# Moving the input norm of a hybrid encoder layer from the loads to the first two q tiles of group B

## Chip, cores, metric

The kernel runs on one core of one Trainium2 chip. The metric is the device time of one execution in microseconds (us), as the median of several runs.

## The reference

One layer of a streaming encoder. It is given 512 prompt tokens and 8 x 16 sample tokens (640 in all) of width 2048, caches of keys and values for the samples, and the weights. What matters for this change is its beginning:

```
def rmsnorm(x, g):
    xf = x.astype(jnp.float32)
    y = xf * lax.rsqrt(jnp.mean(xf * xf, axis=-1, keepdims=True) + EPS)
    return (y * g.astype(jnp.float32)).astype(x.dtype)

qa, ka, va, qb, kb, vb = split_proj(rmsnorm(x, norm_mix) @ w_in)
qb = rope_partial(qb, pos)
kb = rope_partial(kb, pos)
oa = band_attend(...)      # group A: 16 heads, learned bias
ob = band_attend(...)      # group B: 16 q heads, 2 kv heads, sinks
y = merge_and_ffn(x, oa, ob, ...)
```

The projection of a normed row is the projection of the row times its gain, scaled afterwards by one number for each token, r = 1/sqrt(mean(x^2) + EPS). So the projection can begin before r is known, and r is needed only when a projected tile is scaled. Behind the attention follow the output projection, a SwiGLU of width 5632 and a last norm.

## The kernel before

All activations are held with features on the 128 partitions and the 640 tokens along the free dimension, as two halves of 320. `xT` is 16 tiles of 128x640. Each operand of a dense product is split into two fp32r parts, a high one by ScalarE (L168 for weights, L172 for x with its gain) and a low one by VectorE (L169, L173), and each product is three matmuls: high by high (L177), high by low of one side (L178) and of the other (L179). In `dense` (L195) one output tile of 128x640 takes 16 k tiles x 2 halves x 3 = 96 matmuls of 128x320. It accumulates in a buffer of the PSUM pool "dn", of which there are two. A bank group is free for the next output once its result has been taken out. Weights come in chunks of up to 8 k tiles of 128x128: `weights` (L187) takes a raw slot (list WR, two slots), issues the load on SyncE's queue, and splits it into a slot for the high and one for the low part (list WH, four slots, so two chunks).

The program begins with the load loop (L319). It loads the 16 x tiles, splits them (`acts`), and between them loads the weights of k and v of group B (w_in 24 and 25) in three chunks each of 2, 6 and 8 k tiles. The k and v tiles are accumulated together (`dense(first, acts, 2)`), so they hold both "dn" buffers, and follow the loads k tile by k tile.

`input_norm` (L331) makes r: the raw x tiles are squared in place, the squares are added into one tile, TensorE sums them over partitions with a column of ones (L221), six small instructions make the inverse root with a Newton step, and TensorE spreads it over the partitions again (L233), from where ScalarE copies it into `r_mix` (L235). Before the change six of the 16 squares and five adds are GpSimd's (L335, L339), ten squares are ScalarE's (L337), and ten adds VectorE's (L341).

Work beside the dense products is written as generators in a queue ("heads"). `dense` calls `tick` after every six matmuls of an output, which adds `rate` to a counter and runs one step (`pump`) of the queue for each whole number. `rate` is 1.0 at first, 0.8 from the k and v tiles on, and 1.1 from p = 4, where the decoding of the samples joins as a second stream. `input_norm` is the first generator; `drain` (L103) runs it to its end behind the k and v product. The heads of the attention follow in the same queue, two at a time: scores of a pair (L367, L369), softmax, transposes (L289), products with v (L184, L185). Four steps make the scores of a pair, and there are some 18 steps in all. The matmuls of a step never stand ahead of the dense matmul that was written before them (`keep_pace`). For the rest a scheduler places instructions of independent chains on each engine; each engine then works off its queue in order.

After the k and v product come: `proj` (L352), which takes a result out of PSUM and scales it with `r_mix` in one VectorE instruction (L356); `rope` (L503), which zeroes a tile on GpSimd (L505), moves rows by four small DMAs (L507, L508), and adds up on VectorE (L509 to L511); the splits of k; the transposed v (`values`). Then the loop over p runs `project_b` twice (q tiles 26 + t) and `project_a` once (k, q, v of group A), for p = 0 to 3, and `project_a` alone for p = 4 to 7.

The lists S, W, F and others are slots of on-chip memory handed out by `get` and given back by `put`. `qps`, in the changed kernel, is a list of the two PSUM results that wait for their scale.

Of the kernel before, what the change touches and what calls it, by code (L numbers as in the profile page):

```python
# [7 lines left out]
AF = mybir.ActivationFunctionType  # L8
ALU = mybir.AluOpType
# [6 lines left out]
KT = 16  # L16
# [29 lines left out]
def halves(ap):  # L46
    return ap.rearrange("p (a b) -> p a b", a=2)
# [222 lines left out]
def build(nc, tc, io, pools):  # L270
    n = Net(nc, tc, io, pools)
# [26 lines left out]
    def pair(lst, k=TOK):  # L298
        a, b = n.get(lst), n.get(lst)
        return (a, b), (r(a[:, :k]), r(b[:, :k]))  # L300
# [9 lines left out]
    r_mix, cos, sin, kb0, kb1, vb0, vb1 = (n.get("C") for _ in range(7))  # L310
# [6 lines left out]
    xg, acts, xs = [], [], []  # L317
    first = []
# [10 lines left out]
        xs.append(xr)  # L329

    def input_norm():  # L331
        pool = (1, 3, 5, 7, 9, 11)
        for i, x in enumerate(xs):
            if i in pool:
                nc.gpsimd.tensor_tensor(x, x, x, ALU.mult)  # L335
            else:
                nc.scalar.activation(x, x, AF.Square)  # L337
        for i in pool[1:]:
            nc.gpsimd.tensor_tensor(xs[1], xs[1], xs[i], ALU.add)  # L339
        for i, j in ((0, 2), (4, 6), (8, 10), (0, 4), (12, 13), (0, 8), (0, 1), (14, 15), (0, 12), (0, 14)):  # L340
            nc.vector.tensor_tensor(xs[i], xs[i], xs[j], ALU.add)  # L341
        for _ in range(25):
            yield
        n.put("S", *xs)
        for _ in n.rstd_steps({a: [xs[0][:, a * HT:a * HT + HT]] for a in range(2)}, D, r_mix):
            for _ in range(4):
                yield
        n.move("S", "Q", 4)
        dma(out=cos[:80], in_=io["rope"][0])
        dma(out=sin[:80], in_=io["rope"][1])  # L350

    def proj(idx, ps=None):  # L352
        if ps is None:
            ps = n.dense([(io["w_in"][idx, :, k:k + 8], 8) for k in (0, 8)], acts)
        out = n.get("F")
        nc.vector.tensor_tensor(halves(out), ps, halves(r_mix), ALU.mult)  # L356
        return out
# [131 lines left out]
    def heads_of(kind, p, held, *args):  # L489
        ot = n.get("S")  # L490
        left = [2]

        def done():
            left[0] -= 1
            if not left[0]:
                dma(out=(oa_d if kind is prompt_a else ob_d)[p, :, :SP], in_=ot[:, :SP])
                n.put("S", ot)
                for lst, t in held:
                    n.put(lst, t)

        n.add("heads", kind(p, *args, ot, done))

    def rope(x):  # L503
        rot = n.get("S")
        nc.gpsimd.memset(rot[:80], 0.0)  # L505
        for b in (0, 64):
            dma(out=rot[b:b + 8], in_=x[b + 8:b + 16])  # L507
            dma(out=rot[b + 8:b + 16], in_=x[b:b + 8])  # L508
        nc.vector.tensor_tensor(x[:80], x[:80], cos[:80], ALU.mult)  # L509
        nc.vector.tensor_tensor(rot[:80], rot[:80], sin[:80], ALU.mult)  # L510
        nc.vector.tensor_tensor(x[:80], x[:80], rot[:80], ALU.add)  # L511
        n.put("S", rot)
# [170 lines left out]
        n.put("D", o_s, bias, *z, *held)  # L683


    n.add("heads", input_norm())
    ps_k, ps_v = n.dense(first, acts, 2)
    n.drain()
    n.rate = 0.8
    kf = proj(24, ps_k)  # L690
    rope(kf)
    dma(out=io["o_kb"], in_=kf)
    n.split(kf, *kb)
    n.put("F", kf)
    vf = proj(25, ps_v)
    dma(out=io["o_vb"], in_=vf)
    values(vf, [r(x[:, :SP]) for x in (vb0, vb1)])
    ps = n.bank()[:, :P]
# [2 lines left out]
    n.put("F", vf)  # L701

    def project_b(t):
        qf = proj(26 + t)
        rope(qf)
        nc.vector.tensor_scalar(qf, qf, 0.125, None, ALU.mult)
        dma(out=sb_d[:, t], in_=qf[:, SP:])
        qo, qb = pair("Q", SP)
        n.split(qf[:, :SP], *qb)
        n.put("F", qf)  # L710
        heads_of(prompt_b, t, [("Q", x) for x in qo], qb)
# [25 lines left out]
    for p in range(8):  # L737
        if p < 4:
            project_b(2 * p)
            project_b(2 * p + 1)  # L740
        if p == 4:
            while len(n.lists["Q"]) < 4:
                n.pump()
            n.move("Q", "D", 4)
            n.put("D", cos, sin)
            n.streams = (("heads 0", "heads"), ("decode", "decode"))
            n.add("decode", decode_b())
            n.add("decode", decode_a(0))
            n.rate = 1.1
        project_a(p)  # L750
# [24 lines left out]
    for m in range(KT):  # L775
        ps = n.dense([(io["w_out_b"][m], 8)], acts_b)
        if m == 0:
            n.rstd(ssq, 1024, r_b)
        xr, x = n.get("S"), n.get("S")
# [53 lines left out]
    for i, m in enumerate(m for kt in range(8) for m in (kt, kt + 8)):  # L833
        ps = n.dense([(io["w_out_a"][m], 8)], acts_a)
# [355 lines left out]
```

## Time and profile before

| | us |
|---|---|
| median of 3 runs | 2677.78 |
| the runs | 2683.37, 2677.60, 2677.78 |
| the profiled execution | 2685.62 |
| its span in the profile | 2683.8 |

The mean granted clock of TensorE in the profiled execution was 0.989. A row of a timeline reads: start in us from the span's start, duration, engine, line and operation, out<-in with shapes, count, and in brackets the idle time of the engine before it and what ended it. A row of the waits reads: who waited, for whom, us in total, times, longest. A row of the windows reads: stretch, its length, busy time and count of instructions of TensorE's matmuls, its weight loads, VectorE, ScalarE and GpSimd, then the granted TensorE clock, the DMA engines' busy share and GB/s. A merged row ("x4") gives the time from the first start to the last end; instructions of one engine overlap a little, so the spacing from start to start is shorter than the duration of one.

### The profile page before, as it was taken

What the parts mean: (1) busy time and instruction counts of PE and PEld (TensorE: products, weight loads), DVE (VectorE), ACT (ScalarE), POOL (GpSimd) and SP (SyncE); (2) the same over time, 40 slices, a digit from 0 to 9 for tenths busy, and PEclk for the clock granted to TensorE, in tenths of its full rate; (3) what the DMA queues carried; (4) which work ended last, traced back from release to release, by engine and by line L of the source; (5) the groups of instructions that cost most, each with busy time, mean ns of one, the idle gap of its engine ahead of it and who ended that gap; (6) DMA issues with size and microseconds to landing.
All of it is one profiled execution on the core that took longest, in us unless ns stands there. A gap on an engine that the chain in (4) does not pass through costs nothing.

```text
span 2683.8 us, 44823 instructions
## 1 busy us (share of the span) xinstructions
PE 2600.3 (97%) x17565; PEld 2540.1 (95%) x17565; DVE 1925.1 (72%) x2956; ACT 1081.2 (40%) x1759; POOL 789.5 (29%) x564
## 2 busy tenths in 40 slices
PE   7999999999999999999999999999999999999986
PEld 7999999899899999999999999999999899999986
DVE  7555566655866877667676667666678888888897
ACT  4333344434633643333333333333334444444443
POOL 3000000000302223333433433333335434344354
PEclk9999999999999999999999999999999999999998
DMA  5222223333655432332333333333325644444344
GB/s 162 89 72 89 96 66 105 119 120 130 214 188 194 152 123 96 109 117 97 120 104 112 118 104 106 116 106 105 121 96 174 216 132 127 130 133 129 108 114 139
DMA packets 154147, 332.23 MB, mean 124 GB/s; under 512 B 18064, under 2 KB 69264, under 8 KB 153936
## 3 DMA queue, kind: packets, MB, share of 16 engines
q1 hardware_dynamic: 153936, 329.38, 38.9%
q8 instruction: 138, 2.26, 0.4%
q14 instruction: 73, 0.60, 0.1%
HBM read 274.38 MB, written 54.20 MB: 122 GB/s over the span
## 4 chain that ended last, share of the span: by engine, by line
PE 84%; DVE 7%; DMA 3%; issue 3%; ACT 2%; POOL 0%; SPq 0%; DVEq 0%; ACTq 0%; POOLq 0%
PE dn L177 18%; PE dn L179 18%; PE dn L178 17%; PE at L177 9%; PE at L178 8%; PE at L179 8%; DVE W L169 2%; PE at L289 2%; PE at L367 1%; DVE S L908 1%; DMA W<-w_down 1%; DMA S<-act_d 1%; PE at L185 1%; PE at L184 1%; DVE S L1079 1%
## 5 line engine op out<-in xcount | busy, mean ns | idle before, releaser
L177 PE MATMUL dn<-S,W 128*128 128x320 f32 x3694 | 1164.0, 315 | 17.5 <-ACT S L920 7.1
L179 PE MATMUL dn<-S,W 128*128 128x320 f32 x3694 | 1149.6, 311 | 16.6 <-DVE W L169 16.5
L178 PE MATMUL dn<-S,W 128*128 128x320 f32 x3694 | 1148.3, 311 | 2.2 <-DVE S L173 1.1
L168 ACT ACTIVATE W<-W 128x1024 fp32r<-128x1024 f32 (+2 forms) x632 | 608.3, 964 | 1047.3 <-PE dn L178 524.7
L169 DVE TENSOR_TENSOR W<-W,W 128x1024 fp32r<-128x1024 f32 (+2 forms) x632 | 771.0, 1220 | 132.1 <-ACT W L168 128.3
L177 PEld LDWEIGHTS dn<-S,W 128*128 128x128 f32 x3694 | 698.7, 189 | 32.3 <-issue 9.5
L179 PEld LDWEIGHTS dn<-S,W 128*128 128x128 f32 x3694 | 698.4, 189 | 21.9 <-DVE W L169 21.2
L178 PEld LDWEIGHTS dn<-S,W 128*128 128x128 f32 x3694 | 699.0, 189 | 4.5 <-DVE S L173 1.4
L179 PE MATMUL at<-S,W 128*128 128x320 f32 x1594 | 494.0, 310 | 7.0 <-DVE W L169 6.9
L177 PE MATMUL at<-S,W 128*128 128x320 f32 x1594 | 493.4, 310 | 0.1
L178 PE MATMUL at<-S,W 128*128 128x320 f32 x1594 | 493.2, 309 | 0.0
L891 POOL TENSOR_TENSOR W<-W,W 128x1024 f32<-128x1024 f32 (+2 forms) x76 | 163.4, 2150 | 592.5 <-DVE W L169 523.0
L179 PEld LDWEIGHTS at<-S,W 128*128 128x128 f32 x1594 | 299.7, 188 | 9.9 <-DVE W L169 9.8
L177 PEld LDWEIGHTS at<-S,W 128*128 128x128 f32 x1594 | 299.8, 188 | 0.4 <-ACT W L168 0.4
L178 PEld LDWEIGHTS at<-S,W 128*128 128x128 f32 x1594 | 299.9, 188 | 0.0
L908 DVE TENSOR_TENSOR S<-S,dn 128x320 f32<-128x320 f32 x358 | 164.1, 481 | 95.9 <-PE dn L179 94.5
L887 DVE TENSOR_TENSOR W<-W,W 128x1024 f32<-128x1024 f32 (+2 forms) x76 | 133.7, 1759 | 100.3 <-DMA W<-w_up 51.3
L898 POOL TENSOR_TENSOR W<-W,W 128x1024 f32<-128x1024 f32 (+2 forms) x76 | 166.3, 2188 | 110.0 <-DVE W L169 104.6
L908 DVE TENSOR_TENSOR S<-S,at 128x320 f32<-128x320 f32 x262 | 123.2, 480 | 69.2 <-PE at L179 69.2
L248 POOL TENSOR_TENSOR S<-S,S 128x640 f32<-128x640 f32 x40 | 75.4, 1885 | 149.4 <-ACT S L247 148.6
L889 DVE TENSOR_TENSOR W<-W,W 128x1024 f32<-128x1024 f32 (+2 forms) x76 | 82.8, 1090 | 36.7 <-DMA W<-w_gate 24.8
L505 POOL MEMSET S<- 80x640 f32 x9 | 5.7, 629 | 309.9 <-PE at L185 185.8
(146 smaller groups left out, 2285.7 us busy)
## 6 DMA issues: line engine op xcount, KB each, us to landing
W<-w_gate SPq DMA_DIRECT2D x88, 512.0 KB
W<-w_up SPq DMA_DIRECT2D x88, 512.0 KB
W<-w_in SPq DMA_DIRECT2D x66, 512.0 KB
W<-w_down SPq DMA_DIRECT2D x64, 384.0 KB
W<-w_down SPq DMA_DIRECT2D x68, 320.0 KB
act_d<-S SPq DMA_DIRECT2D x66, 320.0 KB
half<-act_d SPq DMA_DIRECT2D x81, 160.0 KB
S<-act_d SPq DMA_DIRECT2D x80, 160.0 KB
```

Of the source, the lines that this page charges most:

```text
L168: self.nc.scalar.activation(hi, src, AF.Identity)
L169: self.nc.vector.tensor_tensor(lo, src, f(hi), ALU.subtract)
L177: mm(out, a[0], b[0], start=first, stop=False)
L178: mm(out, a[0], b[1], start=False, stop=False)
L179: mm(out, a[1], b[0], start=False, stop=last)
L248: (eng or nc.gpsimd).tensor_tensor(ssq, ssq, sq, ALU.add)
L289: nc.tensor.transpose(out, src, n.ident)
L887: nc.vector.tensor_tensor(b12[:, w], b12[:, w], b22[:, w], sub)
L889: nc.vector.tensor_tensor(s6[:, w], b11[:, w], b12[:, w], sub)
L891: nc.gpsimd.tensor_tensor(b11[:, w], b22[:, w], s6[:, w], sub)
L898: nc.gpsimd.tensor_tensor(b21[:, w], b21[:, w], s6[:, w], sub)
L908: add = lambda o, a, b: nc.vector.tensor_tensor(o, a, b, ALU.add)
```

## The change

k and v are copied out of PSUM by ScalarE unscaled, as soon as they are accumulated. Then the two q tiles 26 and 27 are accumulated into the freed buffers, with `input_norm` running beside them at one step for six matmuls. Then k and v are scaled in place by VectorE, and the two q results when `proj` takes them out of PSUM. `input_norm` squares all tiles on ScalarE and adds them one by one into the first on VectorE; GpSimd does nothing in it. The rate behind it is 0.9 instead of 0.8.

```diff
     def input_norm():
-        pool = (1, 3, 5, 7, 9, 11)
-        for i, x in enumerate(xs):
-            if i in pool:
-                nc.gpsimd.tensor_tensor(x, x, x, ALU.mult)
-            else:
+        for i in range(0, KT, 2):
+            for x in xs[i:i + 2]:
                 nc.scalar.activation(x, x, AF.Square)
-        for i in pool[1:]:
-            nc.gpsimd.tensor_tensor(xs[1], xs[1], xs[i], ALU.add)
-        for i, j in ((0, 2), (4, 6), (8, 10), (0, 4), (12, 13), (0, 8), (0, 1), (14, 15), (0, 12), (0, 14)):
-            nc.vector.tensor_tensor(xs[i], xs[i], xs[j], ALU.add)
-        for _ in range(25):
-            yield
-        n.put("S", *xs)
+            if i:
+                n.put("S", xs[i], xs[i + 1])
+            yield
+            for x in xs[max(i, 1):i + 2]:
+                nc.vector.tensor_tensor(xs[0], xs[0], x, ALU.add)
+            yield
+        yield
         for _ in n.rstd_steps({a: [xs[0][:, a * HT:a * HT + HT]] for a in range(2)}, D, r_mix):
-            for _ in range(4):
+            for _ in range(3):
                 yield
+        n.put("S", xs[0], xs[1])
         n.move("S", "Q", 4)
...
+    kf, vf = n.get("F"), n.get("F")
+    for x, ps in zip((kf, vf), n.dense(first, acts, 2)):
+        nc.scalar.activation(halves(x), ps, AF.Identity)
     n.add("heads", input_norm())
-    ps_k, ps_v = n.dense(first, acts, 2)
+    qps = [n.dense([(io["w_in"][26, :, k:k + 8], 8) for k in (0, 8)], acts)]
+    qps.append(n.dense([(io["w_in"][27, :, k:k + 8], 8) for k in (0, 8)], acts))
     n.drain()
-    n.rate = 0.8
-    kf = proj(24, ps_k)
+    n.rate = 0.9
+    nc.vector.tensor_tensor(kf, kf, r_mix, ALU.mult)
     rope(kf)
...
-    vf = proj(25, ps_v)
+    nc.vector.tensor_tensor(vf, vf, r_mix, ALU.mult)
...
     def project_b(t):
-        qf = proj(26 + t)
+        qf = proj(26 + t, qps.pop(0) if qps else None)
```

What this does to the queues is shown at three places. The first is TensorE near the end of the k and v product. `dn_217` and `dn_218` are k and v before, `dn_219` and `dn_220` after, `dn_415` is q tile 26; `at_406` is the norm's sum over partitions; the S tiles are the parts of x, the W tiles those of weights. Before:

```order
L179 MATMUL dn_217<-S_69_207,W_46_159 128x320
L221 MATMUL at_406<-cst,S_11_91 128x1 x6
L177 MATMUL dn_218<-S_69_207,W_54_176 128x320
L178 MATMUL dn_218<-S_70_208,W_54_176 128x320
L179 MATMUL dn_218<-S_69_207,W_55_177 128x320
```

The norm's sum stands ahead of the last 18 matmuls of k and v. After, at the end of the same product:

```order
L178 MATMUL dn_220<-S_73_214,W_54_176 128x320
L179 MATMUL dn_220<-S_72_213,W_55_177 128x320
L177 MATMUL dn_415<-S_12_93,W_80_417 128x320
L178 MATMUL dn_415<-S_13_94,W_80_417 128x320
L179 MATMUL dn_415<-S_12_93,W_81_418 128x320
```

The product runs to its end, and q tile 26 follows. The sum now stands 12 matmuls into q tile 27 (`dn_555`), and the spreading (L233) 18 dense matmuls behind it:

```order
L179 MATMUL dn_555<-S_18_105,W_88_558 128x320
L221 MATMUL at_574<-cst,S_11_91 128x1 x6
L177 MATMUL dn_555<-S_24_117,W_87_557 128x320
L178 MATMUL dn_555<-S_25_118,W_87_557 128x320
L179 MATMUL dn_555<-S_24_117,W_88_558 128x320
```

The second place is VectorE among the loads, from the first chunk of 6 k tiles on (128x768); L173 makes the low parts of x tiles 4 and on, L341 (L339 after) are the norm's adds. Before:

```order
L169 TENSOR_TENSOR W_22_111<-W_20_109,W_21_110 128x768
L341 TENSOR_TENSOR S_11_91<-S_11_91,S_23_115 128x640
L169 TENSOR_TENSOR W_31_129<-W_29_127,W_30_128 128x768
L173 SCALAR_TENSOR_TENSOR S_34_136<-S_32_133,cst,S_33_135 128x640
L173 SCALAR_TENSOR_TENSOR S_37_142<-S_35_139,cst,S_36_141 128x640
L173 SCALAR_TENSOR_TENSOR S_40_148<-S_38_145,cst,S_39_147 128x640
L173 SCALAR_TENSOR_TENSOR S_43_154<-S_41_151,cst,S_42_153 128x640
L341 TENSOR_TENSOR S_32_133<-S_32_133,S_38_145 128x640
L169 TENSOR_TENSOR W_46_159<-W_44_157,W_45_158 128x1024
```

After:

```order
L339 TENSOR_TENSOR S_11_91<-S_11_91,S_17_103 128x640
L169 TENSOR_TENSOR W_22_111<-W_20_109,W_21_110 128x768
L169 TENSOR_TENSOR W_31_129<-W_29_127,W_30_128 128x768
L339 TENSOR_TENSOR S_11_91<-S_11_91,S_23_115 128x640
L173 SCALAR_TENSOR_TENSOR S_34_136<-S_32_133,cst,S_33_135 128x640
L173 SCALAR_TENSOR_TENSOR S_37_142<-S_35_139,cst,S_36_141 128x640
L173 SCALAR_TENSOR_TENSOR S_40_148<-S_38_145,cst,S_39_147 128x640
L173 SCALAR_TENSOR_TENSOR S_43_154<-S_41_151,cst,S_42_153 128x640
L339 TENSOR_TENSOR S_11_91<-S_11_91,S_26_121 128x640
L169 TENSOR_TENSOR W_46_159<-W_44_157,W_45_158 128x1024
```

The scheduler still draws adds of the norm in among the loads, though they are written behind them: six ahead of the last low part of x, where there were five.

The third place is ScalarE from its last split of x (L172) to the end of the k and v product. After the change (L334 squares, L686 copies k and v out of PSUM):

```order
L172 ACTIVATE S_72_213<-S_71_211,cst 128x640
L334 ACTIVATE S_56_181<-S_56_181 128x640
L168 ACTIVATE W_80_417<-W_79_416 128x1024
L334 ACTIVATE S_59_187<-S_59_187 128x640
L168 ACTIVATE W_83_486<-W_82_485 128x1024
L334 ACTIVATE S_62_193<-S_62_193 128x640
L334 ACTIVATE S_65_199<-S_65_199 128x640
L334 ACTIVATE S_68_205<-S_68_205 128x640
L334 ACTIVATE S_71_211<-S_71_211 128x640
L686 ACTIVATE S_74_217<-dn_219 128x640
L686 ACTIVATE S_75_218<-dn_220 128x640
```

Six of the 16 squares and the two chunks of q tile 26 stand between the last split of x and the copy of k; ten squares stand ahead. Before, three squares stood behind the last split of x and no copy out of PSUM.

In both kernels the last 12025 of the 17495 instructions of TensorE are the same sequence of operations on the same kinds of tiles.

## The prediction

> **What bounds the kernel now.** I read the page first (its busy row and the chain that ended last), then who TensorE waited for in the first 130 us, then TensorE's timeline and the windows of that stretch, and last the timelines of the engines that feed it.
>
> ```profile
> PE 2600.3 (97%) x17565; PEld 2540.1 (95%) x17565; DVE 1925.1 (72%) x2956; ACT 1081.2 (40%) x1759; POOL 789.5 (29%) x564
> PE 84%; DVE 7%; DMA 3%; issue 3%; ACT 2%; POOL 0%; SPq 0%; DVEq 0%; ACTq 0%; POOLq 0%
> PE dn L177 <- ACT S L172: 7.1, 1, 7.1
> PE dn L179 <- DVE W L169: 3.8, 2, 2.4
> PE at L221 <- DVE S L341: 2.7, 1, 2.7
> PE dn L177 <- DVE S L356: 0.9, 1, 0.9
> 1200.00:1300.00 100.00, 100.00 (x684) 100.00 (x683) 69.99 (x75) 33.97 (x36) 36.90 (x20) 1.00 0.34 109
> 0.00:17.80 17.80, 8.10 (x34) 7.30 (x34) 9.83 (x10) 10.56 (x14) 5.36 (x7) 1.00 0.80 248
> ```
>
> TensorE is the bound: 97% busy and 84% of the chain. Its matmuls are the same before and after, so only its idle time and its slow clock can change the time. At full clock a dense matmul (128x320) costs 100/684 = 0.146 us, so k and v of B (192 matmuls) are worth 28.1 us. The waits that the change touches all lie before 57 us. In the first 17.8 us 34 matmuls were issued.
>
> ```profile
> 17.87 0.42 PE L179 MATMUL dn<-S,W 128*128 128x320 f32 x1 [2.35 <-DVE W L169]
> 46.94 2.71 PE L221 MATMUL at<-cst,S 128*128 128x1 f32 x12 [2.68 <-DVE S L341]
> 53.39 0.47 PE L179 MATMUL dn<-S,W 128*128 128x320 f32 x1
> 53.65 1.52 PE L233 MATMUL at<-cst,sm 128*128 128x128 f32 x12
> 56.56 0.41 PE L177 MATMUL dn<-S,W 128*128 128x320 f32 x1 [0.89 <-DVE S L356]
> 48.00:52.00 4.00, 4.00 (x17) 4.00 (x18) 0.87 (x6) 0.21 (x1) 0.63 (x1) 0.50 0.60 214
> 710.82 1.39 PE L221 MATMUL at<-cst,S 128*128 128x1 f32 x12
> 716.91 1.45 PE L233 MATMUL at<-cst,sm 128*128 128x128 f32 x12
> ```
>
> The first matmul of q tile 26 starts at 56.56. By then TensorE has done 28.1 us of dense work and the norm's two small groups. At full clock each of those groups occupies 1.25 us (at 710.82 and 716.91 the next matmul follows 1.26 and 1.25 us later). So 56.6 - 28.1 - 2.5 = 26.0 us are lost before q 26: 7 us until the first operands, the rest in waits for VectorE and at half clock (granted clock 0.50 after the 2.68 us wait for the norm's adds).
>
> Why VectorE is late there:
>
> ```profile
> 10.59 2.35 DVE L173 SCALAR_TENSOR_TENSOR S<-S,cst,S 128x640 fp32r<-128x640 f32 x2 [0.46 <-ACT S L172]
> 12.86 0.95 DVE L169 TENSOR_TENSOR W<-W,W 128x768 fp32r<-128x768 f32 x1
> 15.52 2.29 DVE L169 TENSOR_TENSOR W<-W,W 128x768 fp32r<-128x768 f32 x1
> 26.24 2.98 DVE L173 SCALAR_TENSOR_TENSOR S<-S,cst,S 128x640 fp32r<-128x640 f32 x2
> 41.20 0.87 DVE L173 SCALAR_TENSOR_TENSOR S<-S,cst,S 128x640 fp32r<-128x640 f32 x1
> 41.99 3.02 DVE L341 TENSOR_TENSOR S<-S,S 128x640 f32<-128x640 f32 x4
> 44.93 1.21 DVE L169 TENSOR_TENSOR W<-W,W 128x1024 fp32r<-128x1024 f32 x1
> 15.00 2.00 POOL L339 TENSOR_TENSOR S<-S,S 128x640 f32<-128x640 f32 x1
> 25.31 2.42 POOL L339 TENSOR_TENSOR S<-S,S 128x640 f32<-128x640 f32 x1
> 12.86:42.07 29.21, 23.59 (x144) 22.35 (x143) 28.99 (x23) 16.74 (x23) 20.05 (x10) 0.94 0.65 211
> ```
>
> The same split of a weight chunk takes 0.95 us at 12.86 and 2.29 us at 15.52, where a GpSimd add runs from 15.00 to 17.00. A low part of x takes 0.87 us once GpSimd is quiet (41.20) and 1.49 us at 26.24, beside GpSimd. From 12.86 to 42.07 VectorE is never idle, GpSimd is busy for 20.05 us, and the 21 instructions of that stretch take 29.2 us. By the quiet spacings (0.79 for a low part, 0.74 for an add, 0.87 and 1.14 for chunks of 768 and 1024) they are worth 12 x 0.79 + 5 x 0.74 + 2 x 0.87 + 2 x 1.14 = 17.2 us. I put the 12 us between down to GpSimd. [...]
>
> **The change part by part.** First, the queues don't do quite what the words say. ScalarE still has ten squares ahead of the last x split (seven before), VectorE six adds ahead of its last low part (five before). Only the other six squares and the other nine adds stand behind the loads; GpSimd has none. So I walk the load stage with the new queues and quiet durations.
>
> ```profile
> 9.74 1.53 ACT L172 ACTIVATE S<-S,cst 128x640 fp32r<-128x640 f32 x2
> 13.76 0.85 ACT L168 ACTIVATE W<-W 128x768 fp32r<-128x768 f32 x1 [0.85 <-DMA W<-w_in]
> 39.78 1.54 ACT L337 ACTIVATE S<-S 128x640 f32<-128x640 f32 x2 [1.97 <-DVE S L173]
> 42.75 1.99 ACT L168 ACTIVATE W<-W 128x1024 fp32r<-128x1024 f32 x2
> 17.84 0.33 SPq L189 DMA_DIRECT2D W<-w_in  x1
> 0.00:28.00 28.00, 17.60 (x97) 16.54 (x97) 14.99 (x13) 11.47 (x16) 13.25 (x7) 1.00 0.88 279
> ```
>
> *VectorE.* Until 10.59 nothing changes. Low parts of x2, x3 end at 12.2, the first add at 12.9, the first chunk of 768 at 13.8. ScalarE has the second chunk's high part at 14.6 (13.76 + 0.85), so VectorE ends it at 15.5 instead of 17.8. From there stand 12 low parts, 5 adds and 2 chunks of 1024: 12 x 0.79 + 5 x 0.74 + 2 x 1.14 = 15.5 us, so 31.0; short waits for ScalarE make it 32, against 42.07.
>
> *ScalarE.* After 14.6 it has 12 splits of x (0.77), 8 squares (0.72) and 2 chunks (1.0): 17.0 us, so its last x split ends near 31.6. Six squares and q 26's two chunks follow (6.3 us), so it is free at 38.
>
> *Loads.* SyncE issued the last weight chunk of v at 17.84, just as the slot was released by the VectorE split that ended at 17.81; it now does so at 15.5, and the last six x tiles behind it. In 28 us 279 GB/s moved 7.8 MB, and cst, 16 x tiles and the chunks of k and v are 7.8 MB; so x15 is there by 28 even at the old pace, before ScalarE wants it near 30.8. The weights of q 26 are now ahead of the two rope tables on SyncE; the tables are first used past 60, so that costs nothing.
>
> *TensorE.* It has issued the 34 matmuls by 15.5, where it needs the low part of that second chunk. The other 158 take 158 x 0.146 = 23.1 us: 38.7. Each later operand is there first (x4's low part at 17.0, used at 17.6; x8's at 23.3, used at 24.7; x15's at 32, used at 37); only v's last chunk (25.9) comes as it is needed, for which I add 0.1. So k and v end at 38.8, bound by TensorE itself, and several us of slip on VectorE at the end would change nothing.
>
> *The copy of k out of PSUM* stands between k's last matmul (6 matmuls earlier, 37.9 and some tenths to drain) and the first of q 26.
>
> ```profile
> 55.21 0.44 ACT L235 ACTIVATE S<-at 128x320 f32<-128x320 f32 x1 [0.23 <-PE at L233]
> ```
>
> No row shows it at 128x640 from PSUM: between 0.44 (half as wide, from PSUM) and 1.0 (1024 wide), I take 0.8, near the square of that width. It ends at 39.2; q 26 starts at 39.3.
>
> ```profile
> 49.68 0.17 DVE L223 TENSOR_SCALAR sm<-at 128x6 f32<-128x6 f32 x1 [1.67 <-PE at L221]
> 50.75 0.17 DVE L228 SCALAR_TENSOR_TENSOR sm<-sm,sm 128x6 f32<-128x6 f32 x1
> ```
>
> *q 26 and q 27 with the norm beside them.* 192 matmuls are 28.1 us and the norm's groups 2.5, at full clock since nothing makes TensorE wait: the adds end near 41 and are read at 55.2 (12 matmuls into q 27); the small steps between the two groups take 50.92 - 49.68 = 1.2 us, the 18 dense matmuls there 2.6. r_mix is there near 61. The scalings of k and v and the emptying of q 26's bank (0.87 each at most, as a low part of that size) end near 64; the next projection needs that bank at 70. So these, like the other added instructions (VectorE has five more in all, ScalarE eight), lie under the dense work of the q tiles. If that cover were gone the three would cost their 2.6 us on VectorE.
>
> *Behind q 27.* The first head's scores come some 48 matmuls into the next projection, at 77.6; before them VectorE waits for a weight chunk whose slot q 27 frees at 70 (ScalarE 1.0, VectorE 1.1: 72.2) and then does six instructions of up to 0.87 (rope, the emptying of q 27, the split of q) and three of a third of that: up to 78.3. I charge 0.8 for this and for the pace of 0.9, at which heads are denser.
>
> **Sum:** 56.6 - 39.3 = 17.3, less 2.5 for the norm's groups that now come later, less 0.8: 14.0 us gained. The profiled execution took 2685.6 us (span 2683.8), so it would be 2671.6; the median of the runs is 2677.8, 7.8 lower than the profiled one, so the runs would come to 2663.8.
>
> **The rivals.**
>
> ```profile
> 57.00:440.00 383.00, 380.59 (x2677) 360.93 (x2677) 224.02 (x565) 149.18 (x352) 5.36 (x14) 1.00 0.27 86
> 440.00:700.00 260.00, 254.63 (x1717) 234.91 (x1715) 170.85 (x458) 123.05 (x284) 21.26 (x61) 1.00 0.40 126
> PE at L367 <- DVE S L169: 0.5, 1, 0.5
> 100.00:104.00 4.00, 3.10 (x26) 2.25 (x25) 3.52 (x9) 0.63 (x1) 0.00 (x0) 1.00 0.36 113
> 104.00:108.00 4.00, 4.00 (x22) 3.46 (x21) 2.23 (x14) 1.19 (x5) 0.00 (x0) 0.63 0.27 100
> ```
>
> 1. *The denser heads make TensorE wait.* From 57 to 440 it idles 2.4 of 383 us (0.6%), from 440 to 700, where the pace is 1.1, 5.4 of 260 (2.1%). If the first stretch came to the second's share it would idle 7.9, 5.5 more than now: gain 14.8 - 5.5 = 9.3, 2668.5. For it: the pace; against: VectorE is busy for only 224 of 383 us there.
> 2. *VectorE is slow for another reason than GpSimd.* Its stretch then takes 29.2 us and one add more from 12.2, to 42.1; k and v end at 43.9, q 26 starts at 44.2, and the gain is 56.6 - 44.2 - 2.5 - 0.8 = 9.1: 2668.7. Against: 0.95 and 2.29 for one instruction.
> 3. *Waits at the scores lower the clock: slower.* Between 100 and 104 TensorE idled 0.9 us at one pair's scores, and the clock of the next window is 0.63, 3 of its 4 us at half, 1.5 lost: 2.4 us for one pair of heads. This stood at one of the 12 pairs before p = 4. At four to eight more pairs it leaves a gain between 4.4 and -5.2 (no change); from nine more, 21.6 us, the kernel is slower by over 0.2%, and at all 11 it is 26.4 - 14.0 = 12.4 slower, 2690. Against: the other pairs had no such wait at pace 0.8, and 0.9 shortens the time between steps by only a ninth. [...]
>
> **How the numbers follow.** Forecast 0.64; rival 1 0.13; rival 2 0.08; rival 3 as no change 0.10, as slower 0.05. The likeliest time is 2664. The bounds below it: without the half-clock window near 105 (1.5) and without my 0.8 the gain is 16.3, 2661.5, and the runs shown differ by 5.8 among themselves: 2656. Above: both rivals near 2669 with the same spread: 2673. What a measurement tells from no change is 0.2%, 5.4 us. Faster: 0.64 + 0.13 + 0.08 = 0.85; same 0.10; slower 0.05.
>
> **What would show it.** Right: low parts of x near 0.87 us throughout; the last one ended by 33; no wait of TensorE over 0.3 us between 16 and 70 and full clock there; q 26's first matmul near 39, the norm's ones near 55, and the next projection near 70. Wrong: low parts still of 1.5 us (rival 2); q 26 waiting for the copy of k for more than 1 us; TensorE idle at scores or flips between 70 and 430 by over 6 us (rival 1), or several half-clock windows there (rival 3). My walk itself fails if squares ahead of the x splits hold ScalarE up, which would show as VectorE waiting for x splits between 16 and 32.

## The result, and the profile after

| | before | after |
|---|---|---|
| median of 4 runs, us | 2677.71 | 2663.50 |
| lowest and highest run | 2677.60, 2683.37 | 2660.63, 2666.94 |
| profiled execution | 2685.62 | 2662.34 |
| its span | 2683.8 | 2660.6 |

The ratio is 0.9942, 95% interval 0.9924 to 0.9960: 14.2 us less by the medians, where the sum had forecast 14.0 (2663.8, put as 2664).

The busy row and the waits of TensorE in the first 130 us, in the profile after:

```profile
PE 2588.9 (97%) x17565; PEld 2532.0 (95%) x17565; DVE 1916.3 (72%) x2961; ACT 1086.3 (41%) x1767; POOL 765.2 (29%) x553
PE dn L177 <- ACT S L172: 7.5, 1, 7.5
PE at L365 <- DVE sm L367: 0.7, 1, 0.7
PE dn L179 <- DVE W L169: 0.5, 1, 0.5
PE dn L177 <- ACT W L168: 0.2, 1, 0.2
```

The wait for the norm's adds (2.7) and the wait for the scaling (0.9) are gone, and of the waits for VectorE among the loads 0.5 us is left. What follows is VectorE among the loads, from the timeline after:

```profile
14.06 0.96 DVE L169 TENSOR_TENSOR W<-W,W 128x768 fp32r<-128x768 f32 x1 [0.44 <-ACT W L168]
15.67 3.49 DVE L173 SCALAR_TENSOR_TENSOR S<-S,cst,S 128x640 fp32r<-128x640 f32 x4
29.27 2.47 DVE L173 SCALAR_TENSOR_TENSOR S<-S,cst,S 128x640 fp32r<-128x640 f32 x3
```

The instruction that took 2.29 us takes 0.96, four low parts take 3.49 us together, and the last low part ends at 31.7 instead of 42.1. TensorE and ScalarE where k and v end (timelines after; the last two rows are the norm's groups, now inside q tile 27):

```profile
38.60 0.70 ACT L686 ACTIVATE S<-dn 128x640 f32<-128x640 f32 x1 [2.33 <-PE dn L179]
39.14 0.31 PE L179 MATMUL dn<-S,W 128*128 128x320 f32 x1
39.36 0.41 PE L177 MATMUL dn<-S,W 128*128 128x320 f32 x1
55.31 1.39 PE L221 MATMUL at<-cst,S 128*128 128x1 f32 x12
59.28 1.45 PE L233 MATMUL at<-cst,sm 128*128 128x128 f32 x12
```

The last matmul of k and v starts at 39.1, the copy of k takes 0.70 us beside the last matmuls of v, and q tile 26 begins at 39.36 instead of 56.56. No idle time stands before either group of the norm. The granted clock is full from the start of q 26 until 960 us.

### The profile page after: what moved, and what is told of

It is laid out like the page before. It is cut to its first block, busy times and chain, and to the rows that moved or that the text cites. A ratio compares the mean times of both kernels' runs of the same rounds, so it can differ in the third digit from the quotient of the medians.

```text
span 2660.6 us, 44831 instructions
## 1 busy us (share of the span) xinstructions
PE 2588.9 (97%) x17565; PEld 2532.0 (95%) x17565; DVE 1916.3 (72%) x2961; ACT 1086.3 (41%) x1767; POOL 765.2 (29%) x553
## 3 DMA queue, kind: packets, MB, share of 16 engines
q1 hardware_dynamic: 153936, 329.38, 39.1%
## 4 chain that ended last, share of the span: by engine, by line
PE 72%; DVE 6%; DMA 3%; issue 2%; ACT 1%; DVEq 0%; POOL 0%; SPq 0%; ACTq 0%
PE dn L177 15%; PE dn L179 15%; PE dn L178 14%; PE at L177 9%; PE at L178 9%; PE at L179 9%; DVE W L169 2%; DMA S<-act_d 1%; PE at L289 1%; DVE S L910 1%; DMA W<-w_down 1%; DVE S L1081 1%; ACT W L168 0%; DVE S L923 0%; PE at L365 0%
## 5 line engine op out<-in xcount | busy, mean ns | idle before, releaser
L177 PE MATMUL dn<-S,W 128*128 128x320 f32 x3694 | 1161.5, 314 | 14.8 <-ACT S L922 5.7
L179 PEld LDWEIGHTS dn<-S,W 128*128 128x128 f32 x3694 | 697.1, 189 | 15.9 <-DVE W L169 14.7
```

The lines of the kernel that those rows point to most:

```text
L177: mm(out, a[0], b[0], start=first, stop=False)
L179: mm(out, a[1], b[0], start=False, stop=last)
```

## Experiments

"Before" beside a run is the kernel before, run in the same session. Its median was 2679.45 us (14 runs) beside the two kernels that take the causes apart, the pinned one and the one at pace 0.8, 2676.50 (1 run) beside the two with added GpSimd work and the one at half pace, which ran once each, and 2681.62 (7 runs) beside the one with the norm under q 26 alone and the repeat of the changed kernel. A ratio compares the means of the runs. Where a lead or lag "at the n-th matmul" is given, it is the difference of the start times of the n-th matmul record of two traces; all traces have 17565.

### The two causes apart

The change takes GpSimd out of the norm and moves the norm behind the loads. Two kernels do one of these each. The first leaves the place and takes GpSimd out:

```diff
     def input_norm():        # of the kernel before
-        pool = (1, 3, 5, 7, 9, 11)
...
+        for x in xs:
+            nc.scalar.activation(x, x, AF.Square)
+        for x in xs[1:]:
+            nc.vector.tensor_tensor(xs[0], xs[0], x, ALU.add)
         for _ in range(25):
             yield
```

> The kernel before, with the norm where it was, but all 16 squares on ScalarE and all 15 adds on VectorE, as in the changed kernel. Theory (two causes: VectorE is held up by GpSimd among the loads, and TensorE waits for the norm's sum and for r_mix before the two buffers are free): the low parts of x take 0.87 us and k and v end near 39 as in the changed kernel, but then TensorE waits for the adds (near 40.5), the small steps, r_mix and the scaling, and q tile 26 starts near 47 instead of 56.6 and 39.4. About 8 us faster than before, 6 to 7 slower than the changed kernel. Rival (VectorE is slow for another reason than GpSimd): low parts near 1.5 us, q 26 at 56 or later, no gain. Rival (only the wait for r_mix counts): no gain either.

Measured: 2673.37 us, ratio 0.9983 to before (0.9972 to 0.9993). Of the ten runs seven took 2668.5 to 2674.1 us and three 2679.5 to 2680.4, as long as the kernel before; why was not traced. The median gains 6.1 us and the mean 4.9, less than the 8 that I expected. The low parts of x, TensorE's timeline where k and v end, and its windows there:

```profile
15.89 3.49 DVE L173 SCALAR_TENSOR_TENSOR S<-S,cst,S 128x640 fp32r<-128x640 f32 x4
38.60 0.31 PE L179 MATMUL dn<-S,W 128*128 128x320 f32 x1
40.79 1.50 PE L221 MATMUL at<-cst,S 128*128 128x1 f32 x12 [1.88 <-DVE S L335]
43.61 2.82 PE L233 MATMUL at<-cst,sm 128*128 128x128 f32 x12 [1.32 <-DVE sm L228]
47.90 0.60 PE L177 MATMUL dn<-S,W 128*128 128x320 f32 x1 [1.48 <-DVE S L350]
44.00:48.00 4.00, 2.52 (x13) 2.36 (x12) 1.06 (x2) 0.88 (x2) 0.00 (x0) 0.50 0.00 0
48.00:52.00 4.00, 4.00 (x16) 3.96 (x17) 1.11 (x3) 0.94 (x3) 0.00 (x0) 0.50 0.22 55
```

k and v end at 38.6 with quiet low parts, so the loads are as good as in the changed kernel. Then TensorE waits three times, for the adds, the small steps and the scaling, 4.7 us in all, and runs at half clock from 42.2 until 52.4. q 26 starts at 47.9 (47 expected), and at the 250th matmul it lies 6.9 us behind the changed kernel. Both rivals fall: the low parts are quiet, and the gain is not nothing.

The second kernel keeps the new place and gives six squares and five adds back to GpSimd:

```diff
     def input_norm():        # of the changed kernel
+        pool = (1, 3, 5, 7, 9, 11)
         for i in range(0, KT, 2):
-            for x in xs[i:i + 2]:
-                nc.scalar.activation(x, x, AF.Square)
+            for j in (i, i + 1):
+                if j in pool:
+                    nc.gpsimd.tensor_tensor(xs[j], xs[j], xs[j], ALU.mult)
+                else:
+                    nc.scalar.activation(xs[j], xs[j], AF.Square)
...
+                if j in pool:
+                    nc.gpsimd.tensor_tensor(xs[1], xs[1], xs[j], ALU.add)
...
+        nc.vector.tensor_tensor(xs[0], xs[0], xs[1], ALU.add)
```

> The changed kernel, with six of the squares and five of the adds on GpSimd again, as they were before the change. Theory: GpSimd still runs beside the loads (the scheduler draws it in), low parts take up to 1.5 us again, TensorE waits for VectorE between 15 and 35 us, k and v end near 43 instead of 39.1, and nothing waits for r_mix behind them: q 26 at 43 to 44, some 4 us slower than the changed kernel and 10 faster than before. Rival (GpSimd has no part in it): q 26 at 39.4 and the time of the changed kernel.

Measured: 2670.67 us, ratio 0.9966 (0.9953 to 0.9979). VectorE, GpSimd and TensorE in its timelines, and two windows:

```profile
15.48 2.29 DVE L169 TENSOR_TENSOR W<-W,W 128x768 fp32r<-128x768 f32 x1
20.81 1.87 DVE L173 SCALAR_TENSOR_TENSOR S<-S,cst,S 128x640 fp32r<-128x640 f32 x1
38.41 3.79 DVE L173 SCALAR_TENSOR_TENSOR S<-S,cst,S 128x640 fp32r<-128x640 f32 x3
14.96 2.00 POOL L344 TENSOR_TENSOR S<-S,S 128x640 f32<-128x640 f32 x1
47.98 0.41 PE L177 MATMUL dn<-S,W 128*128 128x320 f32 x1
28.00:32.00 4.00, 1.90 (x7) 1.24 (x7) 3.87 (x4) 2.78 (x4) 2.37 (x2) 0.79 0.38 133
32.00:36.00 4.00, 2.93 (x11) 2.93 (x12) 4.00 (x4) 1.93 (x4) 2.44 (x2) 0.50 0.42 114
```

The 2.29 us are back to the digit, with a GpSimd add beside them. The low parts end at 42.2 and q 26 starts at 47.98, not at 43 to 44 as I expected: I left the half clock out. Amid the waits between 28 and 32 the granted clock goes to half and stays there from 30.3 to 37.1 (0.79 and 0.50 in the two windows); TensorE is busy for 5.0 of these 6.8 us, and so some 2.5 us are lost. The rest of the miss is in the waits, 6.4 us between 15 and 33 us. The lag behind the changed kernel is 8.6 us at the 250th matmul, where I expected some 4.

So either half alone brings q 26 from 56.6 to 48, and both together to 39.4. By the lag at the 250th matmul (before 13.5, old place without GpSimd 6.9, new place with GpSimd 8.6), taking GpSimd out is worth 6.6 us at the old place and 8.6 at the new one. Between the places 1.0 us has to be added: by their 250th matmul the kernels with the old place have done the norm's 24 matmuls (2.5 us at full clock), those with the new place 24 dense ones instead (3.5 us). So the new place is worth 5.9 us with GpSimd and 7.9 without it, and both together 14.5: neither half is the change.

### GpSimd's part by itself

Two kernels add GpSimd work to the changed kernel that nobody waits for:

```diff
+    nc.gpsimd.memset(cos, 0.0)                              # gpsimd_adds_added
+    nc.gpsimd.memset(sin, 0.0)
+    for _ in range(16):
+        nc.gpsimd.tensor_tensor(cos, cos, sin, ALU.add)
...
+    for _ in range(40):                                     # gpsimd_memsets_added
+        nc.gpsimd.memset(cos, 0.0)
```

> The changed kernel, with 2 memsets and 16 adds of 128x640 on GpSimd ahead of the norm, on two tiles that hold nothing yet (the rope tables are loaded into them later); nobody waits for their result. They run beside the loads. Theory: the low parts of x and the splits of weights beside them take up to 1.5 and 2.3 us, TensorE waits for VectorE, and q 26 starts at 42 to 46 instead of 39.4. Rival (the loads, not GpSimd, slow VectorE): 0.87 us and 39.4.

> The changed kernel, with 40 memsets of 128x640 on GpSimd ahead of the norm, on a tile that holds nothing yet; nobody waits for them. They only write. [...] Rival (any GpSimd instruction holds VectorE up): low parts of 1.2 us and more, q 26 later.

With the adds, in one run: 2677.38 us against 2676.50 before. VectorE, GpSimd and the first matmul of q 26:

```profile
20.11 7.19 DVE L173 SCALAR_TENSOR_TENSOR S<-S,cst,S 128x640 fp32r<-128x640 f32 x4
20.84 10.02 POOL L334 TENSOR_TENSOR S<-S,S 128x640 f32<-128x640 f32 x5
55.44 0.41 PE L177 MATMUL dn<-S,W 128*128 128x320 f32 x1
```

With the memsets, in one run: 2664.32 us.

```profile
15.58 3.49 DVE L173 SCALAR_TENSOR_TENSOR S<-S,cst,S 128x640 fp32r<-128x640 f32 x4
16.29 3.40 POOL L332 MEMSET S<- 128x640 f32 x5
39.49 0.41 PE L177 MATMUL dn<-S,W 128*128 128x320 f32 x1
```

Sixteen adds of no use take the whole gain away (q 26 at 55.44, beyond the 42 to 46 that I expected). Single low parts take up to 2.2 us, TensorE waits 10.0 us for VectorE instead of 0.5, and the clock is at half from 17.8 to 24.7 and from 34.9 to 45.1. Forty memsets, which keep GpSimd busy for 21 of the 25 us between 7 and 32 but only write, change nothing: four low parts take 3.49 us with and without them, and q 26 starts at 39.49, where I had expected 0.87 us for a low part and 39.4. So with the same loads four low parts take 7.19 us beside the adds and 3.49 beside the memsets: in this kernel GpSimd's adds slow VectorE, and neither the loads nor GpSimd's being busy does. What it is in an add no run shows.

### Is the product of k and v bound by TensorE?

This kernel forces the squares, and so the adds, behind ScalarE's last split of x:

```diff
...
+        for i, ins in act:       # ScalarE's instructions; the condition keeps those on the raw x tiles from input_norm on
+            if i >= at and split and any(...):
+                n.tc.add_manual_dep(ins, split[-1].name, info, reason="behind the loads")
```

> The changed kernel with the squares forced behind ScalarE's last split of x, so that none of the norm's work stands among the loads (in the changed kernel the scheduler draws ten squares and six adds in). Theory: VectorE and ScalarE end their splits some 5 us earlier, but k and v are bound by TensorE itself, so q 26 starts at 39.4 within 0.5 us and the time is the same within 2 us. Rival (the norm's work among the loads still costs): q 26 earlier by 1 us or more.

Measured: 2665.59 us, ratio 0.9944 (0.9930 to 0.9959). The last low part now ends earlier; the first matmul of q 26 hardly moves:

```profile
27.80 0.88 DVE L173 SCALAR_TENSOR_TENSOR S<-S,cst,S 128x640 fp32r<-128x640 f32 x1 [0.45 <-ACT S L172]
39.12 0.41 PE L177 MATMUL dn<-S,W 128*128 128x320 f32 x1
```

VectorE is done with the low parts at 28.7 instead of 31.7, and TensorE gains 0.24 us, less than the 1.0 us by which two executions of the changed kernel differ at this point (39.36 and 38.40). So the norm's work that the scheduler draws in among the loads costs nothing there.

### How much cover does the norm need?

Two kernels shift the norm within the q tiles; one halves its pace, the other doubles it and puts it beside q 26 alone:

```diff
     n.add("heads", input_norm())
+    n.rate = 0.5             # norm_at_half_pace
...
+    n.rate = 2.0             # norm_beside_one_q_tile
     qps = [n.dense([(io["w_in"][26, :, k:k + 8], 8) for k in (0, 8)], acts)]
-    qps.append(n.dense([(io["w_in"][27, :, k:k + 8], 8) for k in (0, 8)], acts))
```

> The changed kernel, with the norm beside q 26 and q 27 at half the pace, so that its sum comes only behind q 27 and r_mix with no dense work to cover it. Theory: q 26 at 39.4 as before; behind q 27 TensorE waits for the small steps, r_mix, the scaling of k and v and the emptying of q 26's bank, about 5 us, and runs at half clock for a window or two: 5 to 9 us slower than the changed kernel from there on. Rival (the cover is not needed, since other work can go ahead): less than 2 us.

> The changed kernel, with the norm beside q 26 alone at twice the pace; q 27 stands behind the scaling again and is projected as in the kernel before. The sum comes 8 k tiles into q 26. Theory (the cover has several us to spare, so half of it suffices): q 26 at 39.4, the adds end near 43 and the sum is read near 46.5 without a wait, the spreading waits about 0.5 us (9 dense matmuls between the two groups instead of 18), no wait for r_mix at the end of q 26, and the time of the changed kernel within 2 us. Rival (the second q tile is needed as cover): TensorE waits for 2 us or more between q 26 and q 27.

At half pace, in one run: 2667.79 us. TensorE behind q 27:

```profile
67.18 1.39 PE L221 MATMUL at<-cst,S 128*128 128x1 f32 x12
70.69 1.73 PE L233 MATMUL at<-cst,sm 128*128 128x128 f32 x12 [2.12 <-DVE sm L228]
74.55 1.33 PE L289 MATMUL at<-cst,S 128*128 128x128 f32 x5 [2.12 <-DVE S L698]
72.00:76.00 4.00, 1.88 (x10) 1.69 (x10) 2.30 (x3) 0.79 (x4) 0.00 (x0) 0.50 0.21 71
```

It waits twice for 2.1 us and runs at half clock from 71.9 to 78.7: 6.2 us behind the changed kernel at the 450th matmul, within the 5 to 9 that I expected (its time lies 4.3 us above the 2663.5 of the changed kernel). The cover is needed. Beside q 26 alone the median is 2663.48 us (changed kernel in the same session 2663.29), and TensorE's waits up to 130 us are these:

```profile
PE dn L177 <- ACT S L172: 7.5, 1, 7.5
PE dn L177 <- ACT W L168: 0.4, 1, 0.4
PE at L365 <- DVE S L169: 0.3, 1, 0.3
```

The spreading did not even wait the 0.5 us that I expected. One q tile is enough cover; the second adds nothing.

### The pace, and the kernel once more

```diff
-    n.rate = 0.9
+    n.rate = 0.8
```

> The changed kernel with the pace behind the norm at 0.8 as before, instead of 0.9. Theory: q 26 at 39.4 and the same lead until 75 us; between 75 and 425 us idle time of TensorE within 1 us of the changed kernel's, and the same time within 2 us. Rival (the denser heads bring part of the gain, as the half-clock window near 105 us is gone): that window comes back and 2 us or more are lost.

Measured: 2662.44 us, ratio 0.9935 (0.9920 to 0.9950). q 26 came at 40.3, 1 us later than in the changed kernel's profile, because of one wait of 1.3 us for a weight split among the loads; idle time between 75 and 425 us was 2.1 us, against 1.3 in the second profile of the changed kernel. No half-clock window came back near 105. So the pace has no measurable part in the time.

> The changed kernel once more, unaltered, to see what differs between two executions of it. Expected: q 26 between 38.9 and 40.4, a lead of 13 to 15 us over the kernel before at 75 us, and a median within 3 us of 2663.5. If the profile's lead grows beyond 75 us by another amount than in the first profile (17 at 300 us, 19 at 1100, 23 at 2200), that growth is a matter of the single execution and not of the change.

Measured: 2663.29 us against 2681.62, ratio 0.9935 (0.9920 to 0.9949). q 26 came at 38.4, half a microsecond earlier than the range that I gave. Its trace stays within 2.8 us of the first one of the changed kernel from the first matmul to the last. The lead over the profile of before is 14.9 us at the 450th matmul and grows behind it as in the first profile: 18.5 us at the 2000th matmul and 22.4 at the 15000th, against 17.5 and 22.6. So that growth does not belong to a single execution of the changed kernel.

## Why the prediction was right

- *VectorE was late because of GpSimd:* shown. Taking it out brings the quiet durations (four low parts in 3.49 us), giving it back brings the long ones back (2.29 us for the second chunk of 768), and adds that nobody needs do the same (7.19 us for four low parts). That all of the 12 us put down to GpSimd would go was my estimate; some 11.4 went: the same 21 instructions take 19.1 us (12.67 to 31.74) instead of 29.2, and VectorE is busy for 17.6 of them instead of 29.0. Rival 2 (another reason) falls.
- *The walk through the load stage:* second chunk of 768 at 15.0 (15.5 forecast), last low part 31.7 (32), last x split on ScalarE 30.6 (31.6), last matmul of k and v at 39.1 (38.8). That end is set by TensorE itself, as the kernel with the pinned norm shows (0.24 us earlier). The one wait there is the one for v's last chunk: 0.50 us at 26.3, where I had added 0.1 and called anything over 0.3 a bad sign. Two slips of the working changed nothing: cst, the x tiles and the chunks of k and v add up to 7.6 MB and not 7.8, and the spread of 5.8 us would have put the upper bound near 2674.8 and not at 2673.
- *The copy of k:* 0.70 us (0.8), q 26 at 39.36 (39.3).
- *The norm under the q tiles:* sum at 55.3 (55.2), spreading at 59.3 (59.1), both without a wait. The two kernels on the cover show that the cover is what makes it free, and that there is twice as much as needed.
- *Less 0.8 for the first scores and the pace:* this term came out with the other sign, and where it fitted in size that was luck. The first scores start at 78.4 without a wait. The changed kernel does wait 0.71 us, but one step later: the next scores wait until VectorE has worked off the first ones (L367 in this kernel), and that stands behind a weight split of 1.23 us.

```profile
79.07 1.23 DVE L169 TENSOR_TENSOR W<-W,W 128x1024 fp32r<-128x1024 f32 x1 [0.64 <-ACT W L168]
78.41 0.95 PE L365 MATMUL at<-S,S 64*128 64x128 f32 x12
80.56 1.51 PE L365 MATMUL at<-S,S 64*128 64x256 f32 x12 [0.71 <-DVE sm L367]
```

Against it stands what the kernel before lost at its own second pair, which its trace showed and I set only into the range: two waits, and then half clock from 105.0 to 108.4, worth 1.7 us. Up to q 26 the lead is 56.56 - 39.36 - 2.5 = 14.7 us (14.8 forecast); at the 1000th matmul (154 us) it is 16.3. So in these two profiles the term is a gain of 1.6 us instead of a loss of 0.8. How much of that is the change's is open. The kernel with the old place and no GpSimd (last two rows) has the same two waits at the same pair as the kernel before (first two rows), and its clock stays full:

```profile
102.93 0.49 PE L367 MATMUL at<-S,S 64*128 64x128 f32 x4 [0.54 <-DVE S L169]
103.65 0.82 PE L367 MATMUL at<-S,S 64*128 64x256 f32 x6 [0.22 <-DVE sm L369]
96.25 0.50 PE L361 MATMUL at<-S,S 64*128 64x128 f32 x4 [0.55 <-DVE S L169]
96.97 0.83 PE L361 MATMUL at<-S,S 64*128 64x256 f32 x6 [0.22 <-DVE sm L363]
```

The pace itself costs nothing that can be measured, so rival 1 falls. Rival 3 fell too: the granted clock is full from 12 to 960 us.
- *The sum:* 14.0 forecast; 14.2 by the medians of the first measurement, 18.3 by those of the last session. The two profiled executions differ by 23.3 us, more than either. Of the part above 16.3 some 6 us arise between the 1000th and the 15000th matmul, for the most part where TensorE has the same sequence in both kernels. The profiled execution of before lay 8 us above its median. All ten other profiles gain 4.4 to 7.5 us on it between the 5540th and the 15000th matmul, all of it in that common sequence, the one with the useless adds too (from 0.7 to 8.1), whose time is not below that of before. So the excess most likely belongs to this one execution; it is not shown, since there is no second profile of the kernel before.

## What to carry to other kernels

Where an engine that feeds the bound has the same instruction at two durations (here 0.95 and 2.29 us), look what runs beside the long one: moving eleven GpSimd instructions to engines with room was worth about half of this change. A reduction that gates a scale need not hold up the product: empty the accumulator unscaled, let the next independent product run, and scale later, with just enough dense work to cover the chain (here one tile of 96 matmuls at double pace did as well as two: 2663.48 and 2663.29 us). Once the starved engine had become the bound here, further clearing in front of it (the pinned norm) brought 0.24 us there and nothing in the time.

## What the runs showed of the hardware

In the kernel with the added adds, low parts of x start at 20.9, 23.0 and 25.1 us and GpSimd's adds at 22.5, 24.6 and 26.7, so one of each every 2.1 us. Undisturbed, low parts follow each other every 0.8 us, and the first adds, at 2.0, 3.6 and 5.2 us, every 1.6. Beside GpSimd's memsets four low parts took 3.49 us, as they did without them.

TensorE's granted clock fell to half where TensorE was far from idle. In the kernel before TensorE had been busy for 3.10 of the 4 us from 100 to 104, and the clock was at half from 105.0. In the kernel with GpSimd at the new place it had been busy for 3.32 of the 4 us from 24 to 28, it was busy for 1.90 of the 4 us from 28 to 32, and the clock was at half from 30.3. The length of a wait alone does not tell these places: in the kernel before the clock was 1.00 from 18 to 25 us, behind the wait of 2.35 us that ended at 17.9, and two waits as long as those ahead of 105.0 (0.55 and 0.22 us, there 0.54 and 0.22) left it at 1.00 in the kernel with the old place and no GpSimd. What makes the clock fall was not shown. Behind the wait of 2.68 us in the kernel before, TensorE worked at half clock for 6.8 us without a pause (46.9 to 53.7), so by an estimate from these 6.8 us that wait cost another 3.4 us; I had left the half clock out of two of the expectations.
